# Layer 1 of a hybrid block: latent query and key products and the linear attention's gates traced ahead of the spatial gating's products

## Chip, cores, metric

One core of one Trainium2 chip. The metric is the device time of one execution in microseconds (us), as the median of several runs; lower is better. Engines: TensorE (PE, weight loads PEld), VectorE (DVE), ScalarE (ACT), GpSimd (POOL), and SyncE (SP), whose queue issues the transfers.

## What is computed

Two layers over 512 latent and 256 context tokens, model width 1024. Each layer projects the normalised input into four groups of mixers, concatenates their outputs, projects again, and runs a gated MLP. Cut to what matters here:

```python
for l in range(DEPTH):                       # DEPTH = 2
    ctx_out = l < DEPTH - 1
    hx = rmsnorm(x, g_pre_mix[l]) * (1.0 + sc1x) + sh1x
    hc = rmsnorm(ctx, g_pre_mix[l]) * (1.0 + sc1c) + sh1c
    in_x = jnp.split(hx @ w_in[l], SPLITS, axis=-1)
    in_c = jnp.split(hc @ w_in[l], SPLITS, axis=-1)
    oa_x = chunk_mlp(in_x[0], ...)           # A: u * (w_sp . rmsnorm(v)), u, v = gelu
    ob_c, ob_x = gla_mixer(in_c[1], in_x[1], ...)   # B: q, k, v, r, gates
    oc_c, oc_x = s5_mixer(in_c[2], in_x[2], ...)    # C: two-way linear recurrence
    od_c, od_x = mla_mixer(in_c[3], in_x[3], ...)   # D: latents cq, ck, attention
    mix_x = jnp.concatenate([oa_x, ob_x, oc_x, od_x], axis=-1) @ w_out[l]
    x = x + gt1x * rmsnorm(mix_x, g_post_mix[l])
    ...                                      # gated MLP with a depthwise conv
return x
```

In layer 1 the context tokens only feed keys, values and states; their outputs are not needed.

## The kernel before

**Products.** Every large matrix product is three fp32r products (lines L199, L200, L201: high·high, low·high, high·low). A weight tile is loaded by SP (`load_w`, L173, tile raw, four buffers), then `split` makes the high part on ACT (L191, tile whi) and the low part on DVE (L192, tile wlo). The results of the mixer stage land in PSUM tiles `pg`, of which there are two.

**Order.** The Python code traces the instructions; a scheduler then fixes one order for each engine when the kernel is built, from the traced order, the buffers and a simulated timeline. On the chip each engine runs its list in that order and waits where an operand or a buffer is not ready. What is traced earlier is placed earlier if it fits, so moving code moves instructions on all engines.

**The mixer stage** (`Net.mixers`) traces, for a layer:
- `mixer_c`, the S5 recurrence (group C). PE products L714 fill V (tile s5v), copied out of PSUM by DVE (L722, one direction) and ACT (L724, the other). DVE then runs it: steps of one multiply and two adds (L735, L737, L738), first on wide tiles of 128x768, then on narrow ones of 128x64, then the block sweep (L753, L760, L762, L763, each in two parts). The last L763 ends the recurrence. DVE L774 and ACT L776 copy the result out, PE products L788 with L786 (transfers L680 and L781 feed them) fill four PSUM tiles, ACT L789 evacuates, L792 applies gelu, PE L798 transposes, ACT L800 evacuates, PE L814 and ACT L816 and DVE L817 and L818 form the gate, and SP L1552 stores the result.
- `ua`, `va` (group A): two products 128x512 and two token-major ones, evacuated with gelu (L1536, L1596) into tile x12; `mixer_a` squares (ACT L990), reduces (DVE L991), normalises (DVE L995), multiplies on PE (L1001, twice) and finishes on DVE (L1003, L1005, twice). SP L1552 stores its result.
- `cq` (two halves) and `ck` (group D's latents), evacuated by ACT L1536 and L1538.
- `mixer_b` up to its first `yield`: the gates of group B. For each of two pairs: PE L845, ACT L848, DVE L849, then ACT L851 (Exp) and L852 (Ln), each with a table load of its own, then DVE L855, scans L856, L858 to L860; at the end L866, L867 and ACT L868.
- `latent_norms` (ACT L1037, PE L1039, DVE L1043 to L1045, POOL L125, PE L145, DVE L1054).
- `q` of group B: two products, evacuated by ACT L1536 into env.q, whose tile is x12 again, the same buffer that mixer_a's u and v use. L1572 moves halves across partitions; ACT L873 and DVE L874 scale it. Then `vb` (three token-major products, ACT L1623) and, behind the stage's first pools, `k` (tile bk, ACT L1536 and L1538, transfers L1572, DVE L879 with ACT L878), `r` and the rest.

Of the kernel before, what the change touches and what calls it, by code (L numbers as in the profile page):

```python
# [90 lines left out]
class Net:  # L91
# [1419 lines left out]
    def mixers(self, l, ctx, md, early=None):  # L1511
        nc = self.nc
        G = (0, 1, 2) if ctx else (0, 1)
        G3 = (0, 1, 2)
# [3 lines left out]
        cq = self.t(mp, [128, 2, T], "cq")  # L1518
        ck = self.t(mp, [128, T], "ck")

        def fm(wv, groups):
            px = pc = None
            if 0 in groups:
                px = self.t(self.psg, [128, 512], "pg")
                self.gemm_fm(wv, KT, self.hrhs, px, None, [g for g in groups if g < 2])
            if 2 in groups:
                pc = self.t(self.psg, [128, 512], "pg")
                self.gemm_fm(wv, KT, self.hrhs, None, pc[:, :256], [2])
            return px, pc


        def half(n, i):
            return self.wsplit(l, ("in", n), i)

        def evac(dst, px, pc, rows=slice(0, 128), func=AF.Copy):
            nc.scalar.activation(dst[:, :NX], px[rows], func)  # L1536
            if pc is not None:
                nc.scalar.activation(dst[:, NX:], pc[rows, :256], func)  # L1538

        def tmajor(name, groups, sink):  # L1540
            wvs = [half(name, q) for q in range(2)]
            for g in groups:
                ps = self.t(self.psg, [128, 512], "pg")
                for j in range(2):
                    js = slice(j * 128, j * 128 + 128)
                    self.mm3(ps[:, j * 256:j * 256 + 256],
                             [((self.hh[g][:, k, js], self.hl[g][:, k, js]),
                               (wvs[k // 4][0][:, k % 4, :], wvs[k // 4][1][:, k % 4, :])) for k in range(KT)])
                sink(g, ps)

        def store(o, k, mix, t0=0):
            nc.sync.dma_start(md[:, o + k, t0:tn], mix[:, t0:tn])  # L1552

        psls, tabs, tables = early or (self.pool("psb", space=PSUM), None, None)
# [8 lines left out]
        env = SimpleNamespace()  # L1563

        def heads(n, x, groups):
            w = 256 * len(groups)
            for hp in range(2):
                px, pc = fm(half(n, hp), groups)
                for hr in range(2):
                    rs = slice(hr * 64, hr * 64 + 64)  # L1570
                    evac(x[rs, 2 * hp + hr], px, pc, rs)
                    nc.sync.dma_start(x[64 - hr * 64:128 - hr * 64, 2 * hp + hr, :w], x[rs, 2 * hp + hr, :w])  # L1572
# [3 lines left out]
        def visit(n):  # L1576
            for _ in range(n):
                next(rest, None)

        with self.pool("mc") as pm:  # L1580
            with self.behind(self.hlast if tables else None):
                for _ in tables or ():
                    pass
            self.mixer_c(l, self.uf[l], lambda k, t: store(4, k, t), pm, pcp, "pc1", ctx)
            if l == 0:
                rest = chain(*(self.mod_pair(p, self.gate) for p in (1, 2)))
            visit(2)
            x12 = self.t(px_, [128, 4, T], "x12")
            x6 = self.t(px_, [128, 1536], "x6")
            ut = x12[:, 0:2]  # L1590
            va = x12[:, 2:4].rearrange("p a t -> p (a t)").rearrange("p (i c) -> p i c", i=6)
            for i in range(2):
                px, pc = fm(half("ua", i), G)
                evac(ut[:, i], px, pc, func=AF.Gelu_apprx_tanh)
                visit(1)
            tmajor("va", G, lambda g, ps: nc.scalar.activation(  # L1596
                va[:, 2 * g:2 * g + 2].rearrange("p i c -> p (i c)"), ps[:], AF.Gelu_apprx_tanh))
            visit(2)
            self.mixer_a(l, ut, va, x6, px_, "pb2", ctx)
            visit(2)  # L1600
            for k in range(2):
                store(0, k, ut[:, k])
            for i in range(2):
                px, pc = fm(half("cq", i), G3 if i else G)
                evac(cq[:, i], px, pc)
                visit(1)
            px, pc = fm(half("ck", 0), G3)
            evac(ck, px, pc)
            visit(2)
            if tabs:  # L1610
                tabs.__exit__(None, None, None)
            mgs = self.pool("mg", side="right")
            pg = mgs.__enter__()
            b = self.mixer_b(l, env, cq[:, 1], pg, ("pb2", "pb1"), ctx)
            next(b)
            visit(2)
            self.latent_norms(l, cq, ck, pg, "pb2", "pb1", ctx)
            visit(4)
            env.q = self.t(px_, [128, 4, T], "x12")
            heads("q", env.q, G)  # L1620
            next(b)
            env.v = vb = self.t(px_, [128, 6, 256], "x6")
            tmajor("vb", G3, lambda g, ps: nc.scalar.copy(  # L1623
                vb[:, 2 * g:2 * g + 2].rearrange("p i c -> p (i c)"), ps[:]))
        pcs.__exit__(None, None, None)
        with self.pool("mb") as env.p:
# [4 lines left out]
            for hp in range(2):  # L1631
                px, pc = fm(half("r", hp), G)
# [174 lines left out]
```

## Time and profile before

| | before |
|---|---|
| median of 3 runs | 1910.93 us (1908.58 to 1912.76) |
| the profiled execution | 1912.24 us |
| its span, first to last instruction | 1910.4 us |
| PE busy | 1775.8 us (93%) |
| DVE busy | 1197.7 us (63%) |
| ACT busy | 776.7 us (41%) |

The profiled execution's time is 1.84 us more than its span and 1.31 us over the median. The 93% is an average over the program: the mixer stage of layer 1 takes a small part of it, about 1186 to 1345 us of the span, and has stretches with much idle time on PE. All times below are from the span's start.

### The profile page before, as it was taken

What the parts mean: (1) busy time and instruction counts of PE and PEld (TensorE: products, weight loads), DVE (VectorE), ACT (ScalarE), POOL (GpSimd) and SP (SyncE); (2) the same over time, 40 slices, a digit from 0 to 9 for tenths busy, and PEclk for the clock granted to TensorE, in tenths of its full rate; (3) what the DMA queues carried; (4) which work ended last, traced back from release to release, by engine and by line L of the source; (5) the groups of instructions that cost most, each with busy time, mean ns of one, the idle gap of its engine ahead of it and who ended that gap; (6) DMA issues with size and microseconds to landing.
All of it is one profiled execution on the core that took longest, in us unless ns stands there. A gap on an engine that the chain in (4) does not pass through costs nothing.

```text
span 1910.4 us, 28205 instructions
## 1 busy us (share of the span) xinstructions
PE 1775.8 (93%) x11256; PEld 1515.4 (79%) x11256; DVE 1197.7 (63%) x2200; ACT 776.7 (41%) x1242; POOL 123.9 (6%) x142
## 2 busy tenths in 40 slices
PE   5899989899989899999999988997989999999996
PEld 2785677679977788888888886886668988888886
DVE  8866734664879853554885775683565765455555
ACT  2433454454753333322322344364444653333332
POOL 0000000000430000000000033000000310000002
PEclk7999998899999999999999988998889899999998
DMA  9457630015623342222564433323102523323341
GB/s 351 140 170 253 200 95 24 28 37 185 204 70 112 109 122 78 88 89 85 183 185 133 143 100 104 115 69 95 33 24 94 187 83 88 110 78 110 86 146 45
DMA packets 94386, 222.14 MB, mean 116 GB/s; under 512 B 10928, under 2 KB 41008, under 8 KB 93232
## 3 DMA queue, kind: packets, MB, share of 16 engines
q1 hardware_dynamic: 94256, 220.36, 37.0%
q8 instruction: 88, 1.44, 0.3%
q14 instruction: 42, 0.34, 0.1%
HBM read 193.35 MB, written 24.08 MB: 114 GB/s over the span
## 4 chain that ended last, share of the span: by engine, by line
PE 71%; DVE 11%; issue 9%; ACT 4%; DMA 2%; POOL 1%; SPq 0%; POOLq 0%; DVEq 0%; ACTq 0%
PE pf L199 16%; PE pf L200 16%; PE pf L201 16%; PE pg L199 3%; PE pg L201 3%; PE pg L200 3%; PE pb L243 1%; DVE wlo L192 1%; PE pd L1161 1%; PE pn L322 1%; DVE z L1215 1%; PE pc L714 1%; ACT whi L191 1%; DMA bk<-bk 1%; DVE nu L389 1%
## 5 line engine op out<-in xcount | busy, mean ns | idle before, releaser
L192 DVE TENSOR_TENSOR wlo<-raw,whi 128x1024 fp32r<-128x1024 f32 (+1 forms) x215 | 252.5, 1175 | 292.4 <-ACT whi L191 289.5
L191 ACT ACTIVATE whi<-raw 128x1024 fp32r<-128x1024 f32 (+1 forms) x215 | 217.4, 1011 | 398.0 <-PE pf L200 340.7
L199 PE MATMUL pf<-hhx,whi 128*128 128x512 f32 (+1 forms) x1032 | 365.8, 360 | 13.3 <-DVE z L1215 6.0
L200 PE MATMUL pf<-hlx,whi 128*128 128x512 f32 (+1 forms) x1032 | 369.1, 359 | 6.1 <-DVE hlx L391 5.9
L201 PE MATMUL pf<-hhx,wlo 128*128 128x512 f32 (+1 forms) x1032 | 366.8, 357 | 0.7 <-DVE wlo L192 0.5
L199 PEld LDWEIGHTS pf<-hhx,whi 128*128 128x128 f32 x1032 | 199.9, 196 | 41.2 <-issue 7.3
L200 PEld LDWEIGHTS pf<-hlx,whi 128*128 128x128 f32 x1032 | 201.8, 196 | 33.6 <-DVE hlx L391 8.9
L201 PEld LDWEIGHTS pf<-hhx,wlo 128*128 128x128 f32 x1032 | 201.8, 196 | 27.0 <-DVE wlo L192 1.5
L199 PE MATMUL pf<-g,whi 128*128 128x512 f32 (+1 forms) x552 | 185.8, 342 | 5.3 <-DVE z L1215 2.9
L201 PE MATMUL pf<-g,wlo 128*128 128x512 f32 (+1 forms) x552 | 187.5, 341 | 0.8 <-DVE wlo L192 0.8
L200 PE MATMUL pf<-g,whi 128*128 128x512 f32 (+1 forms) x552 | 187.8, 341 | 0.0
L1215 DVE SCALAR_TENSOR_TENSOR z<-pf,cols,z 128x511 f32<-128x511 f32 (+1 forms) x264 | 167.9, 656 | 28.3 <-ACT z L1213 25.8
L200 PE MATMUL pf<-hl,whi 128*128 128x256 f32 x432 | 123.0, 286 | 0.4 <-DVE hl L391 0.4
L199 PE MATMUL pf<-hh,whi 128*128 128x256 f32 x432 | 121.5, 286 | 1.6 <-ACT hh L390 1.5
L201 PE MATMUL pf<-hh,wlo 128*128 128x256 f32 x432 | 122.1, 284 | 0.0
L199 PEld LDWEIGHTS pf<-g,whi 128*128 128x128 f32 x552 | 104.7, 192 | 18.8 <-issue 3.7
L201 PEld LDWEIGHTS pf<-g,wlo 128*128 128x128 f32 x552 | 105.8, 192 | 12.2 <-DVE wlo L192 1.0
L200 PEld LDWEIGHTS pf<-g,whi 128*128 128x128 f32 x552 | 105.8, 192 | 11.5 <-DVE g L1265 0.2
L1213 ACT ACTIVATE z<-pf,cols 128x512 f32<-128x512 f32 (+1 forms) x132 | 90.1, 695 | 38.3 <-PE pf L201 29.9
L1294 DVE TENSOR_TENSOR y<-y,pf 128x512 f32<-128x512 f32 (+1 forms) x88 | 44.7, 515 | 73.1 <-PE pf L201 73.1
L125 POOL TENSOR_TENSOR nroy<-nroy,mhalf 128x2 f32<-128x2 f32 x10 | 10.0, 996 | 1202.4 <-DVE nroy L124 894.3
L199 PEld LDWEIGHTS pf<-hh,whi 128*128 128x128 f32 x432 | 82.4, 193 | 3.9 <-ACT hh L390 2.3
(465 smaller groups left out, 3408.5 us busy)
## 6 DMA issues: line engine op xcount, KB each, us to landing
raw<-in_w SPq DMA_DIRECT2D x170, 512.0 KB, 3.5
rawm<-in_wmod SPq DMA_DIRECT2D x64, 512.0 KB, 4.3
raw<-in_w SPq DMA_DIRECT2D x48, 384.0 KB, 3.2
wm<-in_wmod SPq DMA_DIRECT2D x8, 1024.0 KB, 10.4
silu<-in_wmod SPq DMA_DIRECT2D x16, 512.0 KB, 5.6
dx<-g SPq DMA_DIRECT2D x32, 256.0 KB, 2.3
dG<-gt SPq DMA_DIRECT2D x16, 256.0 KB, 2.8
dE<-es SPq DMA_DIRECT2D x16, 256.0 KB, 2.3
```

The source lines that it names most:

```text
L191: nc.scalar.activation(hv, src, AF.Copy)
L192: nc.vector.tensor_tensor(lv, src, hv.bitcast(F32), op=ALU.subtract)
L199: self.nc.tensor.matmul(out, lh, rh, start=i == 0, stop=False)
L200: self.nc.tensor.matmul(out, lh, rl, start=False, stop=False)
L201: self.nc.tensor.matmul(out, ll, rh, start=False, stop=i == n - 1)
L243: self.nc.tensor.matmul(acc[32 * q:32 * q + 2, :], self.ct[:, k, :], halves[q // 2][:, q % 2 * 512:q % 2 * 512 + 512], start=k == 0, stop= ...
L322: self.nc.tensor.matmul(ps[:, j:j + 1], acc[:, k, j * 128:(j + 1) * 128], self.ones[:, 0:1], start=k == 0, stop=k == 1)
L389: nc.vector.scalar_tensor_tensor(u[:], xk, sc, pb, op0=ALU.mult, op1=ALU.mult)
L714: nc.tensor.matmul(ps[:, g * NCH:(g + 1) * NCH], E[:, b * 4 + g, :], U[:, gg, :], start=True, stop=True)
L1213: nc.scalar.activation(z[:, o:o + m], p[:, :m], AF.Identity, bias=b, scale=w1)
L1215: self.last = nc.vector.scalar_tensor_tensor(z[:, o + d:o + d + m - 1], p[:, s:s + m - 1], w, z[:, o + d:o + d + m - 1], op0=ALU.mult, op1 ...
L1294: nc.vector.tensor_tensor(y[:, m, t0:t0 + tw], y[:, m, t0:t0 + tw], ps[:, :tw], op=ALU.add)
```

## The change

A new inner function `latents` holds the products and evacuations of `cq` and `ck`, the opening of the pool `mg` and the first step of `mixer_b` (the gates). For layer 1 it is called ahead of `ua`, `va` and `mixer_a`, and for layer 0 at its old place. Nothing is added to the computation. (Two of the later lines move: L1596 is L1615 in the changed kernel, L1623 is L1631.)

```diff
             visit(2)
+
+            def latents():
+                for i in range(2):
+                    px, pc = fm(half("cq", i), G3 if i else G)
+                    evac(cq[:, i], px, pc)
+                    visit(1)
+                px, pc = fm(half("ck", 0), G3)
+                evac(ck, px, pc)
+                visit(2)
+                if tabs:
+                    tabs.__exit__(None, None, None)
+                mgs = self.pool("mg", side="right")
+                pg = mgs.__enter__()
+                b = self.mixer_b(l, env, cq[:, 1], pg, ("pb2", "pb1"), ctx)
+                next(b)
+                return mgs, pg, b
+
+            if l:
+                mgs, pg, b = latents()
             x12 = self.t(px_, [128, 4, T], "x12")
...
             for k in range(2):
                 store(0, k, ut[:, k])
-            for i in range(2):
-                px, pc = fm(half("cq", i), G3 if i else G)
-                evac(cq[:, i], px, pc)
-                visit(1)
-            px, pc = fm(half("ck", 0), G3)
-            evac(ck, px, pc)
-            visit(2)
-            if tabs:
-                tabs.__exit__(None, None, None)
-            mgs = self.pool("mg", side="right")
-            pg = mgs.__enter__()
-            b = self.mixer_b(l, env, cq[:, 1], pg, ("pb2", "pb1"), ctx)
-            next(b)
+            if l == 0:
+                mgs, pg, b = latents()
             visit(2)
```

What the scheduler makes of it, at three places of layer 1. **First, ACT around the last copies L724**, which feed the recurrence's first step (x: mixer_a's tiles; bg: gates; pb: their PSUM tile; whi: a high part of a weight). - is before, + is the changed kernel:

```order
 L724 COPY s5v_10723<-pc_1568_10846 64x64x4
-L1596 ACTIVATE x_1595_11085<-pg_11213 128x512
-L191 ACTIVATE whi_11390<-raw_11388 128x1024
-L990 ACTIVATE x_1596_11086<-x_1595_11085 128x512
+L848 ACTIVATE bg_11241<-pb_1615_11249,cols_9_80 128x768
+L851 ACT_TABLE_LOAD
+L851 ACTIVATE bg_11241<-bg_11241 128x1536
 L724 COPY s5v_10723<-pc_1570_10857 64x32x4
 L724 COPY s5v_10723<-pc_1570_10857 64x64x4
```

An evacuation, a split and a square stood ahead of the last eight L724; now the second gate evacuation, a table load and the Exp of the first pair stand there.

**Second, DVE.** The recurrence's first steps before (s5v and s5a: its tiles; wlo: a low part):

```order
1450 L735 TENSOR_TENSOR s5a_10875<-s5l_10729,s5v_10723 128x768
1451 L737 TENSOR_TENSOR s5v_10723<-s5v_10723,s5a_10875 128x12x32
1452 L738 TENSOR_TENSOR s5v_10723<-s5v_10723,s5a_10875 128x12x32
1453 L995 TENSOR_TENSOR x_1595_11085<-x_1595_11085,ary_11270 128x1024
1454 L735 TENSOR_TENSOR s5a_10875<-s5l_10729,s5v_10723 128x768
1455 L192 TENSOR_TENSOR wlo_11554<-raw_11551,whi_11553 128x1024
```

and in the changed kernel (bsc, btot: the gates' other tiles):

```order
1448 L735 TENSOR_TENSOR s5a_10875<-s5l_10729,s5v_10723 128x768
1449 L737 TENSOR_TENSOR s5v_10723<-s5v_10723,s5a_10875 128x12x32
1450 L855 TENSOR_TENSOR bsc_11242<-bsc_11242,bg_11241 128x768 x2
1451 L738 TENSOR_TENSOR s5v_10723<-s5v_10723,s5a_10875 128x12x32
1452 L192 TENSOR_TENSOR wlo_11369<-raw_11366,whi_11368 128x1024
1453 L856 SCALAR_TENSOR_TENSOR bg_11241<-brs_11238,bsc_11242 128x768 x2
1454 L735 TENSOR_TENSOR s5a_10875<-s5l_10729,s5v_10723 128x768
1455 L858 COPY btot_11243<-bg_11241 128x12
1456 L859 TENSOR_TENSOR bsc_11242<-bsc_11242,bg_11241 64x768
```

The gates' chain now stands between the first and the second step. At the recurrence's end, DVE before:

```order
1536 L192 TENSOR_TENSOR wlo_12280<-raw_12277,whi_12279 128x1024
1537 L763 TENSOR_TENSOR s5v_10723<-s5v_10723,s5a_10875 128x11x96
1538 L855 TENSOR_TENSOR bsc_11455<-bsc_11455,bg_11454 128x768 x2
1539 L774 COPY s5a_10940<-s5v_10723 64x8x32
```

and in the changed kernel:

```order
1549 L1054 SCALAR_TENSOR_TENSOR cq_10706<-cq_10706,cols_9_80,pb_1647_11543 128x512
1550 L1054 SCALAR_TENSOR_TENSOR cq_10706<-cq_10706,cols_9_80,pb_1647_11543 96x512
1551 L762 TENSOR_TENSOR s5a_10875<-s5l_10729,s5v_10723 128x1408
1552 L763 TENSOR_TENSOR s5v_10723<-s5v_10723,s5a_10875 128x11x128
...
1557 L192 TENSOR_TENSOR wlo_12280<-raw_12277,whi_12279 128x1024
1558 L763 TENSOR_TENSOR s5v_10723<-s5v_10723,s5a_10875 128x11x96
1559 L774 COPY s5a_10940<-s5v_10723 64x8x32
```

All of the gates, the latent norms and the scaling of q that stood behind the last L763 now stand ahead of it, and L774 follows it at once.

**Third, PE between q and vb** (pg_11592: the second q product; pg_11643: the first vb product). Before, L1001 stood far ahead, in the second cq product:

```order
5737 L201 MATMUL pg_11336<-hhx_3543,wlo_11333 128x512
5738 L1001 MATMUL pb_1615_11274<-x_1596_11086,x_1595_11085 64x128 x8
5739 L199 MATMUL pg_11361<-hh_1528_10605,whi_11332 128x256
```

and in the changed kernel:

```order
5865 L201 MATMUL pg_11592<-hhx_3543,wlo_11589 128x512
5866 L1001 MATMUL pb_1639_11483<-x_1620_11295,x_1619_11294 64x128 x8
5867 L1001 MATMUL pb_1640_11494<-x_1620_11295,x_1619_11294 64x128 x8
5868 L1039 MATMUL pb_1641_11507<-ones_70,bsc_11508 128x1 x10
5869 L1039 MATMUL pb_1641_11507<-ones_70,bsc_11521 128x1 x4
5870 L199 MATMUL pg_11643<-whi_11633,hhx_3543 128x256
```

mixer_a's two products L1001 and the latent norms' L1039 now stand behind both q products and ahead of vb.

## Rows read from the trace of the kernel before

**Rows 1.** By stretch: us, each engine's busy us (count); clock, DMA share, GB/s.

```profile
1251.75:1281.30 29.55, 29.14 (x201) 26.04 (x199) 27.14 (x29) 16.41 (x18) 0.00 (x0) 1.00 0.23 63
1281.00:1321.00 40.00, 28.30 (x171) 24.92 (x171) 21.07 (x37) 24.99 (x36) 2.27 (x1) 0.83 0.25 74
```

The engines stand in the order PE, PEld, DVE, ACT, POOL; the first number is the stretch's length.

**Rows 2.** ACT in order of time: start, us, instruction, idle before and releaser.

```profile
1212.93 2.19 ACT L724 COPY s5v<-pc 64x128 f32<-64x128 f32 x8 [1.10 <-PE pc L714]
...
1247.41 0.90 ACT L848 ACTIVATE bg<-pb,cols 128x768 f32<-128x768 f32 x1 [0.69 <-PE pb L845]
1248.33 1.28 ACT L851 ACT_TABLE_LOAD   x1
1249.62 1.49 ACT L851 ACTIVATE bg<-bg 128x1536 f32<-128x1536 f32 x1
...
1252.42 1.48 ACT L852 ACTIVATE bg<-bg 128x1536 f32<-128x1536 f32 x1
```

**Rows 3.** DVE in the recurrence: its first instruction, two of its waits, its last.

```profile
1215.16 0.96 DVE L735 TENSOR_TENSOR s5a<-s5l,s5v 128x768 f32<-128x768 f32 x1 [1.79 <-ACT s5v L724]
...
1224.50 0.75 DVE L1003 SCALAR_TENSOR_TENSOR x<-pb,cols,x 128x512 f32<-128x512 f32 x1 [0.81 <-PE pb L1001]
...
1253.94 0.96 DVE L855 TENSOR_TENSOR bsc<-bsc,bg 128x768 f32<-128x768 f32 x1 [2.80 <-ACT bg L852]
...
1278.81 1.25 DVE L763 TENSOR_TENSOR s5v<-s5v,s5a 128x1056 f32<-128x1056 f32 x1
```

**Rows 4.** DVE behind the recurrence, in order of time.

```profile
1279.97 1.82 DVE L855 TENSOR_TENSOR bsc<-bsc,bg 128x768 f32<-128x768 f32 x2
1281.71 3.57 DVE L774 COPY s5a<-s5v 64x256 f32<-64x256 f32 x8
1285.31 3.41 DVE L856 TENSOR_TENSOR_SCAN bg<-brs,bsc 128x768 f32<-128x768 f32 x2
...
1293.62 0.95 DVE L860 TENSOR_TENSOR bg<-bsc,btot 64x768 f32<-64x768 f32 x1
...
1309.06 2.11 DVE L874 SCALAR_TENSOR_TENSOR x<-x,bsc 128x512 f32<-128x512 f32 x3 [3.42 <-ACT bsc L873]
...
1318.98 1.40 DVE L1054 SCALAR_TENSOR_TENSOR cq<-cq,cols,pb 128x512 f32<-128x512 f32 x2
1320.29 0.68 DVE L818 TENSOR_TENSOR s5a<-s5a,s5u 128x512 f32<-128x512 f32 x1
```

**Rows 5.** PE behind the recurrence, in order of time.

```profile
1283.43 1.40 PE L788 MATMUL pc<-s5e,s5a 128*96 128x128 f32 x6 [2.09 <-ACT s5a L776]
...
1307.14 1.19 PE L798 MATMUL pc<-cst,s5v 96*128 96x96 f32 x8 [2.17 <-ACT s5v L792]
...
1311.56 2.82 PE L145 MATMUL pb<-cst,dry 128*128 128x128 f32 x12
1314.17 3.71 PE L814 MATMUL pc<-s5u,s5e 128*128 128x512 f32 x8
```

**Rows 6.** ACT behind the recurrence, in order of time.

```profile
1302.75 0.58 ACT L789 COPY s5v<-pc 96x512 f32<-96x512 f32 x1 [4.02 <-PE pc L788]
...
1303.88 1.28 ACT L792 ACT_TABLE_LOAD   x1
...
1312.34 0.48 ACT L800 COPY s5u<-pc 128x384 f32<-128x384 f32 x1
```

**Rows 7.** The chain that ended last, merged: start, us, what.

```profile
1321.00 2.00 DMA dmixr<-s5a
...
1324.06 4.57 DMA bk<-bk
```

**Rows 8.** PE alone by stretch: us, busy (count), granted clock, DMA share, GB/s.

```profile
1254.73:1268.68 13.95, 13.71 (x114) 1.00 0.22 58
1283.67:1287.08 3.41, 3.41 (x18) 0.50 0.03 5
1392.89:1406.55 13.66, 10.73 (x45) 0.50 0.17 53
```

## The prediction

> **What bounds the kernel now.** I read the page first (PE is busy 93% of the span), then the busy time by stretch of layer 1's mixer stage, since the change moves instructions there alone. Up to 1281 us PE is the bound: in the last 29.55 us of that time it works 29.14, at full clock [rows 1]. From 1281 to 1321 it is not: PE works 28.3 us of 40 and its mean clock is 0.83 [rows 1]. There one chain decides, the end of the S5 recurrence on DVE and what hangs on it. DVE starts the recurrence at 1215.16, when ACT has made the last copies L724, and ends it with L763 at 1280.06 [rows 3]; 3.37 us later PE starts L788 [rows 5]; L789, L792, L798, L800, L814, L816 to L818 follow one another until DVE ends L818 at 1320.97 [rows 4 to 6]; then the chain of waits goes through the store of s5a (2.00 us) and, behind it on SP's queue, the transfer of bk (4.57 us) [rows 7]. I find no slack behind that, so what moves L818 moves the end of the program one for one. The question is therefore: when does DVE end the recurrence, when does PE arrive at L788, and how long is the way from L788 to L818.
>
> **1. The recurrence starts later.** The last L724 wait for their PE products L714 [rows 2]. On PE these stood behind ua, va and 10 rows of cq: 58 matmuls of 128x512 at some 0.23 us and 96 of 128x256 at 0.12 (13.95 us over 114) [rows 8], 24.8 us. In the new order cq, ck, two sets of L845 (about 1.5 us each) and 19 rows of ua stand ahead: 91 at 0.23, 48 at 0.12 and 3 us, 29.7 us. So L714 is about 4.8 us later, at 1217.7 instead of 1212.9. ACT has L848 (0.90), a table load (1.28) and L851 (1.49) ahead of those copies [rows 2]; L848 can start when the L845 just ahead of L714 is done, near 1216.4, so these three end near 1220.0 and the copies (2.19) at 1222.2. The first step moves from 1215.2 to 1222.2: **+7.0**.
>
> On the table load a rule of the skill would give more. The trace has L851 0.01 us behind the end of its load, so a switch costs 1.28 us on ACT [rows 2]. The Trainium skill, "ScalarE: Activation LUTs", section "What ACT_TABLE_LOAD costs", counts 1.38 us of drain beside a load of about the same length; by it the start, and the forecast, would be 1.4 us later. The trace shows no such gap here, and the sum goes by the row.
>
> **2. DVE has more to do before the recurrence ends.** From 1215.16 to 1280.06 DVE waited 6.9 us in five waits (0.81 to 2.80) [rows 3], so its list takes 58.0. The new list of that stretch also holds what stood behind L763: the second pair of gates with its decay, L855 (1.74 to the next start), then L856 to the last L860, from 1285.31 to 1294.57 less one split of 1.12: 8.1 [rows 4], together 9.9; the scaling of q, L874, 2.80; the norms L1054, 1.40 and 1.01 for ck, and 0.64 for their short rows; one split more, 1.2; mixer_a's two reductions with L124, 1.5, which stood ahead of the first step; and less two L849 (2.0), which now stand ahead of it. Sum 16.5. The order rows show that nothing of this can be stepped over. It waits once where I can see it: L855, the third instruction, needs L852, which ACT ends a load and 1.48 us after the copies, 1.2 us after DVE has done its first two. So L763 ends at 1222.2 + 1.2 + 58.0 + 16.5 = 1297.9, less about 0.9 as neighbours overlap by 0.05 to 0.1 us (1.82 us for two L855 whose successor starts after 1.74 [rows 4]), 1297.0. **+17.0** against 1280.06. The DVE's old waits of 6.9 us are used up in this: without them it would be +24.
>
> **3. PE runs dry behind q.** The new env.q is tile x12 again, so ACT can evacuate the first q product only when mixer_a is done with its x12: the second L1005 and the store of its result. Both q products fill both buffers of pg, and L1001, which needs DVE's L995, stands behind them on PE. Before, all that was over 14 us before q came. Now q ends near 1251.5 as before (PE's work up to there is the same). Of DVE's 74.5 us, about 46 lie ahead of the second L1005 (six wide steps, both pairs of gates, six splits, mixer_a): 1223.4 + 46 = 1269.5 or, with the overlaps, 1268.9. The store lands about 2.0 later (as a store of this size does [rows 7]), ACT evacuates, and vb's first product starts near 1271.6. **PE stands still for about 20 us** but for L1001 and L1039. From there vb and the first half of k take 29.55 us less the two L845 that stood among them (3.1), plus the L145 rows now there (1.3): 27.8 [rows 1], and 1.7 more if its clock is at half for one stretch of 3.41 us after the stop, as it was at 1283.67 after PE had waited [rows 5, 8]. PE arrives at L788 at 1299.4 to 1301.1. The other side, DVE's L763 plus 3.37, is at 1300.4. They tie. I take 1300.7 for L788: **+17.3** against 1283.43.
>
> **4. The way from L788 to L818 gets shorter.** It takes 37.54 us now (1283.43 to 1320.97). What leaves it: L1037 between L789 and the gelu table, 1303.88 - 1302.75 less a copy's 0.58, 0.55 [rows 6]; L873 with its table load and L878, which made the eight L798 and four L800 take 5.68 us (1307.14 to 1312.82 [rows 5, 6]) where eight small products and four copies alternating at 0.48 with PE between them need about 4.1, 1.6; L145 between L800 and L814, 1314.17 - 1312.82, 1.35 [rows 5, 6]; L1054 between L817 and the last L818, 1.2 of its 1.40 [rows 4]. Sum 4.7. L1039 stood there too, but the last two groups of L788 are fed by SP's transfers, which are issued as L788's groups release their buffers and move along, so I count nothing for it (at most 1.9). The clock can give back up to 1.7 if L788 now starts at full clock [rows 8], and I take none: PE waits there as before. **-4.7.**
>
> **5. What costs nothing.** ACT has a table load more for ua's gelu, hidden in idle time, and one ahead of the second L878 pair, inside ACT's long wait for bk. The weight splits and loads stay ahead of their products. SP's stores of mixer_a's result stand behind later weight loads, which need splits that DVE does before L1005; they wait for nothing longer than L1005 itself.
>
> **Sum.** +17.3 - 4.7 = +12.6 against the profiled execution: 1912.24 + 12.6 = 1924.8. That execution is 1.31 over the median of its runs, so the median comes out at 1910.93 + 12.6 = 1923.5; with the 0 to 1.9 of L1039 and the clock on the low side I say **1923**.
>
> **The rivals.** *PE is the later side* (22 in 100). After 20 us with little to do PE's clock stays low for longer: the longest half-clock stretch I looked at lasts 13.66 us [rows 8]. Then vb loses 6.8 us, PE reaches L788 at 1306, 5 later, and the time is 1928. For it: PE's stop is long; against it: vb is dense work, and the dense work of the mixer stage stays at full clock [rows 1]. The Trainium skill, "TensorE: Matmul & The Clock Gate", section "What's actually happening", has the clock throttled when PE idles and released by activity; by that rule a short low stretch as in my sum is the expected case, and the rows agree in that 1283.67 follows a wait. *Only the chain gets shorter* (7 in 100, the other side). Here the scalar engine's gates don't hold the copies and DVE's waits swallow the gates: the first step at 1215.2, 16.5 - 8.7 (6.9 and the 1.8 ahead of the first step) = 7.8 later at L763. Less 4.7, less 1.9 for L1039, less 1.7 of clock at L788 and 3.4 at L814, where L145 and L814 run from 1311.56 at half speed (2.82 for 12 small products [rows 5]): -3.9, 1907. It decides from the point where L763 slips by less than 8; against it speaks that DVE's order is fixed and that the last L724 stand behind L851. *It evens out* (7 in 100): L763 slips by 8 to 9 and the way shortens by as much, 1910 to 1912. *Half of it* (8 in 100): DVE's list is only partly in the way, 1914 to 1919.
>
> **How the numbers follow.** The forecast, 1919 to 1926, has 56 in 100. The range from 1914 to 1929 takes in the half case and most of the PE case and leaves out the two on the fast side and the PE case's tail, some 18 in 100. A measurement of this kernel can tell about 0.2%, 3.8 us, from no change. Faster by more than that 0.07, within it 0.08, slower 0.85.
>
> **What would show it.** In the changed kernel's trace: the first L735 near 1222 and the last L763 near 1297, DVE with few waits between; PE idle before vb's first product, released by ACT's evacuation of q, from about 1251 to 1271; L788 near 1301; 33 us from there to L818. If L763 comes before 1288 my step 2 is wrong; if L788 waits for PE's own products and not for L776, the PE case holds; if L879 does not move with L818, the one-for-one claim is wrong.

## The result, and the profile after

The changed kernel takes 1924.97 us (median of 8 runs, 1918.55 to 1930.35); the kernel before, beside it, 1912.99 (8 runs, 1908.58 to 1917.03). The ratio is 1.0061 [1.0041, 1.0080]: slower by 12.0 us. The prediction was 1923, 1914 to 1929. The profiled execution of after took 1919.88 us, its span 1918.1.

The program ahead of the stage is the same code in both kernels, but the point at which the stage begins differs by up to 9 us from one execution to the next. So positions in the stage are compared by their distance from a mark: the start of PE's first L703 in layer 1, which stands ahead of everything that the change moves (1189.96 in before, 1188.21 in after).

ACT at the start of the recurrence (start, us, engine, line, operation, out<-in, form, count, idle before and releaser; compare [rows 2]):

```profile
1214.88 0.90 ACT L848 ACTIVATE bg<-pb,cols 128x768 f32<-128x768 f32 x1 [2.98 <-PE pb L845]
1215.80 1.28 ACT L851 ACT_TABLE_LOAD   x1
1217.10 1.49 ACT L851 ACTIVATE bg<-bg 128x1536 f32<-128x1536 f32 x1
1218.61 2.16 ACT L724 COPY s5v<-pc 64x128 f32<-64x128 f32 x8
1220.79 1.28 ACT L852 ACT_TABLE_LOAD   x1
1222.09 1.48 ACT L852 ACTIVATE bg<-bg 128x1536 f32<-128x1536 f32 x1
```

The eight copies that feed the first step stand behind the gate's evacuation, a table load and the Exp. DVE, in order of time (compare [rows 3, 4]):

```profile
1220.81 0.96 DVE L735 TENSOR_TENSOR s5a<-s5l,s5v 128x768 f32<-128x768 f32 x1 [3.97 <-ACT s5v L724]
...
1223.61 1.83 DVE L855 TENSOR_TENSOR bsc<-bsc,bg 128x768 f32<-128x768 f32 x2 [1.24 <-ACT bg L852]
...
1253.85 1.20 DVE L995 TENSOR_TENSOR x<-x,ary 128x1024 f32<-128x1024 f32 x1
...
1265.87 0.69 DVE L1005 TENSOR_TENSOR x<-x,x 128x512 f32<-128x512 f32 x1
...
1295.45 1.25 DVE L763 TENSOR_TENSOR s5v<-s5v,s5a 128x1056 f32<-128x1056 f32 x1
...
1329.88 0.69 DVE L818 TENSOR_TENSOR s5a<-s5a,s5u 128x512 f32<-128x512 f32 x1
...
1338.34 1.83 DVE L879 TENSOR_TENSOR bk<-bk,bsc 128x768 f32<-128x768 f32 x2 [5.46 <-DMA bk<-bk]
```

The first step to the end of L763 took 64.90 us before and takes 75.89 now, with the gates and mixer_a's end in between. PE (compare [rows 1, 5]):

```profile
1268.90 1.87 PE L1039 MATMUL pb<-ones,bsc 96*128 96x1 f32 x8 [0.78 <-ACT bsc L1037]
1270.63 0.56 PE L199 MATMUL pg<-whi,hhx 128*128 128x256 f32 x1
...
1300.49 0.60 PE L788 MATMUL pc<-s5e,s5a 128*96 128x128 f32 x4
...
1320.68 3.07 PE L798 MATMUL pc<-cst,s5v 96*128 96x96 f32 x16 [3.89 <-ACT s5v L792]
1323.68 4.98 PE L814 MATMUL pc<-s5u,s5e 128*128 128x512 f32 x8
```

vb's first product starts at 1270.63, right behind PE's last L1039, and PE comes to L788 without a wait of its own, 3.79 us behind the end of L763. ACT ahead of that point:

```profile
1262.80 0.84 ACT L1037 ACTIVATE bsc<-ck 96x768 f32<-96x768 f32 x1 [0.63 <-DVE bg L860]
...
1268.22 0.63 ACT L1037 ACTIVATE bsc<-cq 96x512 f32<-96x512 f32 x1 [4.06 <-PE pb L1039]
1268.75 2.42 ACT L1536 ACTIVATE x<-pg 64x512 f32<-64x512 f32 x4
```

So the stop ends by way of the gates' last L860 on DVE, L1037 on ACT and L1039 on PE; the evacuation of q (L1536, into x12) stands behind the last L1037. By stretch, in the manner of [rows 1]:

```profile
1251.00:1270.00 19.00, 10.46 (x60) 9.33 (x58) 18.50 (x33) 5.68 (x9) 0.00 (x0) 0.68 0.27 83
```

In before, the stretch that begins at about the same distance from the mark (61.8 us, here 62.8) has PE at work for 29.14 us of 29.55. Here it works 10.46 of 19.00, and DVE 18.50 of them.

### The profile page after: what moved, and what is told of

Read it like the earlier page. It is cut to its first block, busy times and chain, and to the rows that moved or that the text cites. A ratio compares the mean times of both kernels' runs of the same rounds, so it can differ in the third digit from the quotient of the medians.

```text
span 1918.1 us, 28202 instructions
## 1 busy us (share of the span) xinstructions
PE 1778.5 (93%) x11256; PEld 1516.4 (79%) x11256; DVE 1197.0 (62%) x2200; ACT 779.0 (41%) x1243; POOL 124.0 (6%) x142
## 4 chain that ended last, share of the span: by engine, by line
PE 70%; DVE 12%; issue 9%; ACT 4%; DMA 3%; POOL 1%; SPq 0%; POOLq 0%; DVEq 0%; ACTq 0%
PE pf L199 16%; PE pf L200 16%; PE pf L201 16%; PE pg L199 3%; PE pg L201 3%; PE pg L200 3%; DVE wlo L192 1%; PE pb L243 1%; PE pd L1161 1%; PE pn L322 1%; DVE z L1215 1%; ACT whi L191 1%; DVE nu L389 1%; DVE hlx L391 1%; PE pc L714 1%
## 5 line engine op out<-in xcount | busy, mean ns | idle before, releaser
L1215 DVE SCALAR_TENSOR_TENSOR z<-pf,cols,z 128x511 f32<-128x511 f32 (+1 forms) x264 | 168.0, 656 | 28.3 <-ACT z L1213 25.8
L1213 ACT ACTIVATE z<-pf,cols 128x512 f32<-128x512 f32 (+1 forms) x132 | 90.1, 695 | 38.3 <-PE pf L201 29.9
## 6 DMA issues: line engine op xcount, KB each, us to landing
wm<-in_wmod SPq DMA_DIRECT2D x8, 1024.0 KB, 10.2
```

Source lines behind the costliest of these rows:

```text
L1213: nc.scalar.activation(z[:, o:o + m], p[:, :m], AF.Identity, bias=b, scale=w1)
L1215: self.last = nc.vector.scalar_tensor_tensor(z[:, o + d:o + d + m - 1], p[:, s:s + m - 1], w, z[:, o + d:o + d + m - 1], op0=ALU.mult, op1 ...
```

## The experiments

Positions as differences from before in distance from the mark (one profiled execution each, us, to 0.1), and the medians (n runs) against runs of before taken beside them, whose medians were 1912.93 for the first four experiments, 1913.71 for flip_exp and dve_load and 1913.11 for the rest:

| kernel | first L735 | end of L763 | first L788 | end of L818 | end of span | median (n) | ratio [95%] |
|---|---|---|---|---|---|---|---|
| after | +7.4 | +18.4 | +18.8 | +11.3 | +9.4 | 1924.97 (8) | 1.0061 [1.0041, 1.0080] |
| after_again | +7.4 | +18.4 | +18.8 | +11.3 | +13.5 | 1930.08 (6) | 1.0069 [1.0043, 1.0096] |
| gates_back | +3.7 | -9.6 | -9.5 | -5.6 | +0.1 | 1912.14 (12) | 0.9995 [0.9979, 1.0012] |
| q_flip | +7.4 | +17.5 | +17.6 | +11.7 | +9.8 | 1921.44 (12) | 1.0044 [1.0024, 1.0064] |
| gates_pool | +7.4 | +19.2 | +19.8 | +19.8 | +17.4 | 1929.94 (5) | 1.0094 [1.0071, 1.0117] |
| exp_behind | +5.2 | +12.5 | +16.8 | +14.1 | +11.6 | 1923.52 (7) | 1.0061 [1.0037, 1.0085] |
| flip_exp | +5.2 | +14.5 | +15.4 | +8.1 | +6.1 | 1920.11 (12) | 1.0031 [1.0012, 1.0050] |
| dve_load | 0.0 | +28.3 | +28.2 | +21.3 | +20.5 | 1936.60 (6) | 1.0109 [1.0078, 1.0141] |
| back_flip | +3.7 | -3.2 | -3.0 | +3.0 | +5.2 | 1920.00 (12) | 1.0034 [1.0019, 1.0049] |
| late_norms2 | 0.0 | 0.0 | 0.0 | -5.6 | +5.7 | 1917.74 (12) | 1.0013 [0.9998, 1.0027] |
| late_norms | 0.0 | 0.0 | 0.0 | -5.6 | +13.0 | 1927.56 (8) | 1.0058 [1.0031, 1.0084] |

**after_again: the changed kernel once more**, with no edit.

> The changed kernel once more, unaltered. Theory: the order on each engine is fixed, so the last L763 again ends within 1 us of 1296.7 relative to the same start of the stage, PE stands still before vb, and L788 starts within 2 us of 1300.5; what differs from run to run is where PE's half-clock stretches fall. Time 1920 to 1930, ratio to before 1.004 to 1.008. If instead L763 or the PE stop moved by several us between two profiles, the account from one profile would not hold.

DVE of this second execution, to be held against the rows of after:

```profile
1226.41 0.96 DVE L735 TENSOR_TENSOR s5a<-s5l,s5v 128x768 f32<-128x768 f32 x1 [3.97 <-ACT s5v L724]
...
1301.06 1.25 DVE L763 TENSOR_TENSOR s5v<-s5v,s5a 128x1056 f32<-128x1056 f32 x1
...
1335.48 0.69 DVE L818 TENSOR_TENSOR s5a<-s5a,s5u 128x512 f32<-128x512 f32 x1
```

From the first L735 to the end of L818 both take 109.76 us. The two executions differ by 5.6 us ahead of the mark and by 4.1 behind the stage. So these two profiles of the stage agree to the hundredth, and what scatters is the rest of the program. Why the profiled execution of after shows only 7.6 us over that of before and the medians 12.0 is seen in the same way: the stage alone gave +11.3, and the rest of that execution was 3.7 shorter than in before.

Behind the stage it is PE's clock that differs. From 175 to 230 us behind the mark, PE in after and then in after_again (stretch, busy us and count, clock, DMA share, GB/s):

```profile
1363.21:1418.21 55.00, 44.31 (x367) 0.72 0.08 28
...
1368.82:1423.82 55.00, 46.24 (x352) 0.60 0.08 24
```

Up to there the two executions run alike, and behind L818 the lower clock level was granted for 62.8 us in all in after and for 77.0 in after_again.

**gates_back: only cq and ck are early, the gates are traced where they were** (on after):

```diff
                 b = self.mixer_b(l, env, cq[:, 1], pg, ("pb2", "pb1"), ctx)
-                next(b)
                 return mgs, pg, b
...
                 mgs, pg, b = latents()
+            next(b)
             visit(2)
```

> cq and ck ahead of ua and va as in the changed kernel, but the gates (the first step of mixer_b) traced where they were before. Theory (the gates' DVE rows and their Exp ahead of the last L724 are what delays the recurrence): first L735 back to 1214 to 1216, L763 back to within 3 us of 1280, time within 4 us of before (1908 to 1916). Rival (moving the latent products ahead of mixer_a is enough, since q then meets mixer_a's x12): PE still stands some 10 us or more behind q and the time is over 1918.

The time is that of before: with the early gates gone, the loss is gone, and moving the latent products alone costs nothing that these runs show. The positions were not as expected: the first L735 is at 1218.74 instead of 1214 to 1216, and L763 ends at 1270.40, far ahead of 1280. DVE:

```profile
1269.14 1.25 DVE L763 TENSOR_TENSOR s5v<-s5v,s5a 128x1056 f32<-128x1056 f32 x1
...
1314.55 0.69 DVE L818 TENSOR_TENSOR s5a<-s5a,s5u 128x512 f32<-128x512 f32 x1
...
1336.43 1.83 DVE L879 TENSOR_TENSOR bk<-bk,bsc 128x768 f32<-128x768 f32 x2 [1.98 <-DMA bk<-bk]
```

The recurrence ends 9.6 us earlier than in before, of which 5.6 are left at L818 and 0.4 at the second pair of L879 (1336.43 less its mark, 1189.87, is 146.56, against 147.01). This order does not show what an earlier recurrence alone is worth, since most of the gates' work on DVE now stands behind it: the last L860 ends at 1302.53, and the chain goes on from there through L1037 and L1039 to L814 and L818.

**q_flip: env.q keeps the buffer, but its halves are exchanged** (on after), so that the first q product is evacuated into the half of x12 that mixer_a is done with first:

```diff
-            env.q = self.t(px_, [128, 4, T], "x12")
+            env.q = x12[:, ::-1] if l else self.t(px_, [128, 4, T], "x12")
```

> The changed kernel with env.q in the same tile x12 but in reversed head order, so that the first q product goes into the half that held va, which is free once L1001 has read it; nothing else is altered. Theory (DVE's list sets the end of the recurrence, PE only ties): vb starts about 8 us earlier, near 1262.5, PE waits in front of L788, L763 stays near 1296.7 and L788 near 1300; the time is that of the changed kernel, -2 to 0 us. Rival (PE's stop behind q is what costs): PE reaches L788 8 us earlier and the time falls by 5 to 8 us, to about 1917 to 1920.

PE:

```profile
1264.95 0.56 PE L199 MATMUL pg<-whi,hhx 128*128 128x256 f32 x1
...
1297.43 0.68 PE L788 MATMUL pc<-s5e,s5a 128*96 128x128 f32 x4 [1.24 <-ACT s5a L776]
```

vb starts 78.5 us behind the mark instead of 82.4 (3.9 earlier, where 8 were expected), so that PE now waits at L788 for ACT's L776. L788 comes only 1.3 earlier, and L818 and the end of the span 0.4 later. The median is 3.5 lower than after's and 5.1 lower than that of the 14 runs of after and after_again together (1926.6), but the intervals of the ratios overlap, and the rival's 5 to 8 us are not ruled out by the times. The positions decide: with 3.9 us of PE's stop gone, the recurrence holds L788 nearly where it was. Most of the stop is still there, so this run does not show what it would be worth to remove all of it.

**exp_behind: the Exp of the first pair is held behind the last L724** (on after):

```diff
-                                nc.scalar.copy(dst[:, s0:s0 + c1 - c0, :], sv)
+                                self.s5in = nc.scalar.copy(dst[:, s0:s0 + c1 - c0, :], sv)
...
-            nc.scalar.activation(pair, pair, AF.Exp, scale=-1.0)
+            with self.behind(self.s5in if l and hp == 0 else None):
+                nc.scalar.activation(pair, pair, AF.Exp, scale=-1.0)
```

> The changed kernel with one more rule for the scheduler: layer 1's first Exp of the gates (L851, here L852) may only come behind the recurrence's last copies L724 on ACT. Theory (the copies wait for the Exp and its table load, 2.8 us of the 5 to 7 us by which the recurrence starts later): from PE's first L703 to DVE's first L735 some 30 us instead of 32.6; L763 earlier by 1 to 3 us, and the time 0 to 3 us under the changed kernel's. If the start does not move, L714's later place on PE was all of it.

ACT, DVE and PE (L1002, L1004 and L1537 are L1001, L1003 and L1536 of after):

```profile
1217.79 2.16 ACT L724 COPY s5v<-pc 64x128 f32<-64x128 f32 x8 [0.62 <-PE pc L714]
...
1290.90 1.26 DVE L763 TENSOR_TENSOR s5v<-s5v,s5a 128x1056 f32<-128x1056 f32 x1
...
1261.43 2.88 PE L1002 MATMUL pb<-x,x 128*64 128x128 f32 x16 [5.66 <-DVE x L1004]
...
1272.27 2.44 ACT L1537 ACTIVATE x<-pg 64x512 f32<-64x512 f32 x4 [2.58 <-DMA dmixr<-x]
...
1299.44 0.61 PE L145 MATMUL pb<-cst,dry 128*128 128x128 f32 x4
1299.88 0.60 PE L788 MATMUL pc<-s5e,s5a 128*96 128x128 f32 x4
```

The copies now wait for PE's L714 alone. The first step comes 2.2 us earlier and L763 ends 5.9 earlier (1 to 3 were expected), but L788 only 2.0 earlier: it starts 7.7 us behind the end of L763, right behind PE's L145. Here PE is the later side, and ACT's evacuation of q does wait for the store of mixer_a's result out of x12. The gain is lost on the way: from L788 to L818 it takes 34.9 us here and 30.1 in after, so that L818 ends 2.8 later than in after. So the two sides are nearly a tie at L788, as the prediction had it: q_flip brings PE forward, exp_behind brings DVE forward, and neither moves L788 by more than 2 us.

**flip_exp: both edits together.**

> The changed kernel with both the reversed head order of q (q_flip) and the Exp held behind the last L724 (exp_behind). q_flip alone brought PE to L788 earlier and left L763; exp_behind alone brought L763 5.9 us forward and L788 only 2. Theory (DVE's list and PE tie at L788, so only both together move it): L763 near +102 to +103 from the first L703, L788 3.4 behind it at +106, L818 near +137 instead of +142.4, the time 3 to 7 us under the changed kernel's. Rival (something else holds L788): L788 stays at +110 or later.

```profile
1294.17 1.26 DVE L763 TENSOR_TENSOR s5v<-s5v,s5a 128x1056 f32<-128x1056 f32 x1
...
1299.68 0.82 PE L788 MATMUL pc<-s5e,s5a 128*96 128x128 f32 x6
```

With both, L763 ends 3.9, L788 starts 3.4 and L818 ends 3.2 us earlier than in after, and the median is 4.9 lower. Unlike either edit alone, it moves L788 and L818 together. The positions are 2 to 3 us later than expected (the scheduler moved other instructions too). What remains over before is 6.4 us between the medians and 6.1 at the end of the span. By the positions the recurrence starts 5.2 later and DVE's list from the first step to the end of L763 takes 9.3 longer, while the way from L788 to L818 is 7.3 shorter.

**gates_pool: three of the gates' element-wise instructions (L855, L859, L860) on GpSimd** instead of DVE (on after; they are L856, L860 and L861 in this kernel, and L995 is L996):

```diff
-                tt(gm, gm, ga, op=ALU.subtract)
+                gt = nc.gpsimd.tensor_tensor if l else tt
+                gt(gm, gm, ga, op=ALU.subtract)
...
-                tt(gm[hi], gm[hi], ga[hi], op=ALU.subtract)
-                tt(gac[hi], gm[hi].rearrange("p (c s) -> p c s", s=64),
+                gt(gm[hi], gm[hi], ga[hi], op=ALU.subtract)
+                gt(gac[hi], gm[hi].rearrange("p (c s) -> p c s", s=64),
```

> The changed kernel with layer 1's L855, L859 and L860 (12 instructions, some 10.9 us of DVE) on GpSimd instead of DVE. Theory: DVE's list ahead of L763 is shorter by about 10 us, L763 near 1286 to 1288; L1005 and so vb come earlier too; the time falls by 6 to 12 us against the changed kernel, to 1912 to 1918. Rival (GpSimd is too slow: 0.8 to 0.9 us for 256 columns, so some 2.7 us each, 32 us in all, and the scans L856 wait for it): DVE waits in the recurrence, L763 stays at 1294 or later and the time stays within 3 us of the changed kernel or above.

The gates' tile on GpSimd (durations in ns: shortest, median, longest), the wait on PE (sum, count, longest in us), and DVE:

```profile
L856 POOL TENSOR_TENSOR bsc<-bsc,bg x4: 1843/1922/2832, 1224.4 to 1255.8; 128x768 f32<-128x768 f32 x4
...
PE pb L1002 <- DVE x L996: 14.9, 1, 14.9
...
1288.16 0.68 DVE L1006 TENSOR_TENSOR x<-x,x 128x512 f32<-128x512 f32 x1
...
1297.00 1.25 DVE L763 TENSOR_TENSOR s5v<-s5v,s5a 128x1056 f32<-128x1056 f32 x1
```

The gain did not come. An L855 takes 1.84 to 2.83 us there against 0.92 on DVE (two in 1.83); DVE's next instructions wait for it, mixer_a's last L1005 comes 21.5 us further from the mark than in after, and L763 does not come earlier at all. The work left DVE but stayed in its chain.

**dve_load: the recurrence's wide multiplies L735 made three times** (on before), which adds 13.6 us of instructions to DVE's list ahead of L763:

```diff
-            tt(q, lam[:, m - 1].unsqueeze(2).to_broadcast([128, 2, n, 32]),
-               src.unsqueeze(1).to_broadcast([128, 2, n, 32]), op=ALU.mult)
+            for _ in range(3 if l and n > 1 else 1):
+                tt(q, lam[:, m - 1].unsqueeze(2).to_broadcast([128, 2, n, 32]),
+                   src.unsqueeze(1).to_broadcast([128, 2, n, 32]), op=ALU.mult)
```

> The kernel before with DVE work added to the recurrence and nothing else: each of the seven wide multiplies L735 of layer 1 is done three times, which gives the same values; 14 more instructions at 0.97 us, 13.6 us. Theory (DVE's list up to L763 sets L788 and all behind it, one for one, once its 6.9 us of waits are filled): L763 7 to 10 us later (+97 to +100 from the first L703 instead of +90), L818 as much later, the time 6 to 10 us over before. Rival (there is slack behind the recurrence): L763 moves but the time stays within 3 us of before.

DVE (L856 is L855 of before, L764 its L763):

```profile
1252.56 1.83 DVE L856 TENSOR_TENSOR bsc<-bsc,bg 128x768 f32<-128x768 f32 x2 [2.73 <-ACT bg L853]
...
1276.86 0.95 DVE L856 TENSOR_TENSOR bsc<-bsc,bg 128x768 f32<-128x768 f32 x1
...
1305.46 1.26 DVE L764 TENSOR_TENSOR s5v<-s5v,s5a 128x1056 f32<-128x1056 f32 x1
```

L763 ends 28.3 us later, twice what was added and some three times what was expected. Both pairs of gates, whose second pair stands behind L763 in before [rows 4], now stand ahead of it, as in the changed kernel, but here without any code having been moved. A likely reason is that the scheduler sees the recurrence end late and fills in other work ahead of it; that was not shown. So this run is not a delay of DVE alone. For the claim on what L818 is worth, that does not matter: L818 +21.3, end of span +20.5, median +22.9.

**back_flip: gates_back and q_flip together.**

> gates_back with the reversed head order of q_flip: neither the gates' DVE rows ahead of the recurrence's end nor PE's stop behind q. Theory: PE's stop of 2.5 us for ACT's evacuation of q and the half-clock stretch behind it (some 5 to 9 us at half speed) go, and as PE is what this arrangement waits for, the time falls by 2 to 6 us against gates_back, to about 1906 to 1910. Rival (the chain through L818 or the transfer of k sets the end): within 2 us of gates_back.

The median is 7.9 us above gates_back's, where a gain was expected. From gates_back to back_flip the end of L763 goes from +80.5 to +86.9 behind the mark and L818 from +125.4 to +134.0: one changed buffer gave DVE another order. An edit that helped on one order cost on another.

**late_norms2 and late_norms: the latent norms and the scaling of q traced behind k** (on before; late_norms puts the norms behind r), to shorten the way from L788 to L818 alone. The edit of late_norms2:

```diff
-            self.latent_norms(l, cq, ck, pg, "pb2", "pb1", ctx)
+            if l == 0:
+                self.latent_norms(l, cq, ck, pg, "pb2", "pb1", ctx)
...
-            next(b)
+            if l == 0:
+                next(b)
...
             heads("k", env.k, G3)
+            if l:
+                next(b)
+                self.latent_norms(l, cq, ck, pg, "pb2", "pb1", ctx)
             next(b)
```

> The kernel before, with layer 1's latent norms and the scaling of q (second step of mixer_b) traced behind the k products instead of ahead of q. Theory (step 4: L1037, L1039, L873, L878, L145 and L1054 lengthen the way from L788 to L818, and nothing else moves): L763 stays at its distance from the first L703 (90 us), the way falls from 37.5 to 30 to 32 us, the time by 4 to 7 us to about 1906 to 1909. Rival (the work only moves behind L818, where it stands in the way again, PE's L1039 and L145 ahead of L885): the way is shorter but the time stays within 3 us of before.

> As late_norms2, but the latent norms traced behind the r products and only the scaling of q behind the k products. Theory: the way is 30 to 32 us as there; L1039 and L145 now come behind the linear attention's own products, so the time falls by 4 to 7 us unless the latent attention waits for the normalised latents, which would give back 2 us or more.

Of late_norms2, DVE, PE, and PE by stretch behind the stage (stretch, busy us and count, clock, DMA share, GB/s); the last line is the same stretch of before:

```profile
1314.99 0.69 DVE L818 TENSOR_TENSOR s5a<-s5a,s5u 128x512 f32<-128x512 f32 x1
...
1325.55 1.83 DVE L879 TENSOR_TENSOR bk<-bk,bsc 128x768 f32<-128x768 f32 x2 [7.55 <-DMA bk<-bk]
...
1343.24 2.29 PE L1039 MATMUL pb<-ones,bsc 96*128 96x1 f32 x20
...
1357.00 2.56 PE L145 MATMUL pb<-cst,dry 128*128 128x128 f32 x12
...
1345.00:1420.00 75.00, 64.16 (x607) 0.70 0.07 22
...
1345.00:1420.00 75.00, 64.34 (x608) 0.80 0.08 27
```

The way from L788 to L818 shrinks from 37.5 to 32.0 us, as expected: with these instructions gone from it, it is that much shorter without any wait removed. But the time does not follow. L879 keeps 3.5 of the 5.6 us, and from the end of L818 to the end of the span it is 600.7 us (608.0 in late_norms) against 589.5; two profiles of one code differed by 4.1 behind the stage, so most of this is more than scatter. In late_norms2 the rival came true, and by more than it had said: PE's two groups of L1039 (2.29 and 1.86 us) and the latent attention's L1088 (2.92) now stand ahead of and between the products L885, L145 (2.56 and 1.16) follows behind them, and the last copy of their results (ACT L886) ends 4.5 us later from the mark than in before, though L879 had been 3.5 earlier. Most of this ran at the lower clock; from 1345 to 1420 the granted clock is 0.70 against 0.80. In late_norms the latent attention's first value products (L1097) start at 1391.7 us against 1359.0 in before, which fits the wait of the attention for the norms that the expectation allowed. How much of either loss is the order and how much the clock was not measured apart.

## Why the prediction was right

The time (1924.97 against 1923) and the sum (+12.0 between medians, +12.6 predicted against the profiled execution) came out. The 2.0 that the time was over are the size by which the base moved: before's median was 1910.93 over 3 runs and 1912.99 over 8.

- **Step 1, the start of the recurrence:** +7.4, predicted +7.0. exp_behind shows the scalar engine's part: 2.2 us of it were the Exp ahead of the copies, and the rest is mostly that L714 stands later on PE, as the prediction had it. The row on the table load held: L851's load ends at 1217.08 and its ACTIVATE starts 0.02 us later, so nothing of the 1.38 us drain that the Trainium skill, "ScalarE: Activation LUTs", section "What ACT_TABLE_LOAD costs", adds to a load of this length (1.28) is seen here.
- **Step 2, DVE's list:** L763 ends +18.4, predicted +17.0. The wait at L855 is 1.24, predicted 1.2. From the first step to the end of L763 it is +11.0 where the step's terms gave +10.0: the list was 0.9 shorter than summed, and three waits of 0.29, 0.41 and 1.26 that the order did not show cost 2.0. (The five old waits add up to 6.9 as the step says, but the shortest is 0.38 and not 0.81.)
- **Step 3, PE dry behind q:** vb from 1270.63, predicted 1271.6; PE at L788 at 1300.49, predicted 1300.7. The mark stood 1.8 us earlier in this execution, so in distance vb came 0.8 later than predicted and L788 1.5 later (+18.8 against +17.3). The other 0.7 is mostly the clock: from vb to L788 it took 29.9 us against 29.1, with the first 4.4 us of vb at the lower level, 2.2 us lost where some 1.3 had been counted. The stop was there, but its end came another way than the step has it. The store of mixer_a's result landed at 1268.58 and ACT began the evacuation of q at 1268.75, so the first q buffer was free near 1269.9; PE was then still at L1039, which the step had named and not priced, until 1270.8. The two ways end within about 1 us of each other, so that the forecast of vb came out is in part luck. In exp_behind the shared x12 is what ACT waits for.
- **Step 4, the way from L788 to L818:** 30.08 us, 7.5 shorter, predicted 4.7. This is the mis-sized step, and what it missed is two of its own terms, both set at nothing. The first two groups of L788 ran faster, so that the third could start 1.6 sooner (the clock, "up to 1.7", taken as none), and the groups behind them came 1.4 sooner with L1039 gone ("at most 1.9", counted as nothing). The terms that were counted held: L1037 0.53 (0.55), the stretch from L798 to the first L816 2.76 (1.6 and 1.35), L1054 1.18 (1.2). The end points set by rows were right, and the choice inside them was not: PE alone behind the start of L788 in after (stretch, busy us and count, clock, DMA share, GB/s), where [rows 8] have 0.50 in the same place, and then its wait for the next transfer:

```profile
1300.50:1303.50 3.00, 3.00 (x30) 1.00 0.00 0
...
1309.10 0.61 PE L786 MATMUL pc<-s5t,s5u 128*96 128x128 f32 x2 [3.65 <-DMA s5t<-dK]
```

  I took no gain of clock "since PE waits there as before". It doesn't: with the tie it comes to L788 from dense work. And I reasoned for L1039 that SP's transfers pace the last two groups. PE does wait for them, but the first such wait ends 8.6 us behind the start of L788 against 10.2 before, and the rest follows from there with L1039 gone.

- **The errors cancelled:** steps 1 to 3 gave 1.5 too little and step 4 took 2.8 too little, which leaves L818 at +11.3 where the sum had +12.6. So the sum is 1.3 off and not the 0.6 by which the medians differ from it, and that it is no more is luck.
- **One for one behind L818:** in after both pairs of L879 move by 11.4, as L818 does (the first row of it stands above), and dve_load agrees over 21 us. For delays the claim holds within the scatter behind the stage, though gates_pool's end (+17.4) is 2.4 short of its L818 (+19.8). For gains the runs are divided. From after to flip_exp L818 comes 3.2 earlier and the end of the span 3.3. But gates_back has -5.6 at L818 and +0.1 at the end, late_norms2 -5.6 and +5.7; both also moved work to behind L788 or L818, and that work was then the next limit. So "no slack behind that" held for delays; that a gain at L818 passes on was not shown for the order of before.
- **The rivals:** *only the chain gets shorter* fell, since DVE's order held the gates ahead of L763. (Its 3.4 at L814 was also misread: before ran L145 at half clock from 1311.56, but L814, from 1314.40 on, at full clock.) *PE is the later side* came in part: by the prediction's own sign, L788 in after waits for nothing but PE's own products. PE is later by some 0.4 us, since L788 starts 3.79 behind L763 where it starts 3.42 behind it in q_flip, waiting for L776. Its condition came as well, a low clock of nearly 14 us (below), but not its price: all but 4.4 us of that lay ahead of vb.

What the runs show of the cause: without the early gates the loss is gone (gates_back); with them, and with the Exp moved behind the copies and vb 6.4 us earlier than in after (from 1266.86, 76.0 behind the mark), 6.4 of the 12.0 us are left (flip_exp); and an order in which L763 ends later because DVE holds more ahead of it delays the end by nearly as much as it delays L818 (dve_load). No run has the early gates without any stop of PE, so how the 12.0 us divide between DVE's list and PE's stop is not shown beyond the near tie.

## What to carry to other kernels

When work is traced ahead of a recurrence that one engine runs in a fixed order, sum what that engine now holds ahead of the recurrence's end; that the work had been hidden before says nothing, since it had been hidden behind that point. Look which buffers the moved code meets: here products that wait for late work on DVE (L1001, L1039), and a tile handed from one mixer to another, left PE, which had been full, with little to do for some 19 us. Where two such obstacles tie, look at both: here either edit alone moved L788 by 2 us or less, and both together moved it by 3.4. A term between two bounds should be taken at the value that the mechanism gives at the new place, not at zero because it can't be proved.

## What was not expected of the hardware

PE's granted clock while it had only mixer_a's and the latent norms' small products (L1001, L1039), and in the first products of vb (stretch, PE's busy us and count, clock, DMA share, GB/s):

```profile
1250.00:1260.00 10.00, 4.14 (x22) 0.83 0.18 52
1260.00:1270.00 10.00, 7.33 (x42) 0.57 0.32 105
1270.00:1275.00 5.00, 5.00 (x24) 0.50 0.48 105
1275.00:1280.00 5.00, 5.00 (x45) 0.99 0.01 3
```

The lower level, 1.2 GHz, was granted for nearly 14 us (about 1261 to 1275). Before it fell PE had been busy 4.14 us of 10, with waits between its products and a shorter low stretch already among them (0.83). It then stayed low while PE was busy 7.33 us of 10 with L1001 and L1039, and through 4.4 us of vb's dense products: a product of vb took 0.21 us there and 0.12 behind 1275. GpSimd took 2 to 3 times as long as DVE for the same 128x768 subtraction (1.84 to 2.83 us against 0.92).
